# Attention: the squares for RMSNorm move from VectorE to ScalarE, and its factor is formed in three steps

## The chip, the cores and the metric

The kernel runs on one core of a Trainium2 chip. The metric is the device time in microseconds of one execution. PE is the matrix engine (TensorE), DVE is VectorE, ACT is ScalarE, POOL is GpSimd, and SP issues transfers.

## The reference

Two layers of a decoder run on 2048 prompt tokens and 64 sample tokens (8 sequences of 8), of 1024 features. The even layer projects its input, mixes half of it by pooling, and passes the other half through differential attention of four heads. The odd layer is gated linear attention. All is float32. The part that matters here is the attention of the prompt, its norm and its gate:

```python
p = softmax(sc)                          # [b, heads, 2, query, key], causal
a = p[:, :, 0] - lam_full * p[:, :, 1]
o = einsum('bhqk,bkhe->bqhe', a, v)      # 128 values a head
...
o = o * rsqrt(mean(o * o, -1) + 1e-5) * subln_w * (1 - lam_init)
mix = concat([pool_out * silu(pg), o * silu(ag)])
y = layer_norm(ALPHA * x + mix @ w_out)
```

## The kernel before

The program has three parts in time: the even layer's projection (`project_even`), the attention, and the odd layer (`Odd`). Float32 products with weights are done as three products of exact parts each (`mm3`, lines 51 to 53), with the parts formed by `split` (lines 40 to 45).

Attention (`class Attention`) goes by tiles of 128 queries. For each of 16 tiles t and each head h there is a unit, and `units` (line 572) lays them out: heads 0, then 1, then 2 and 3 in turn. A unit has two halves, and the second half (`pv`) comes two units after the first (`scores`), so that the engines overlap.

`scores` (line 459) has PE form the scores of two maps (the two softmaxes of differential attention) in pieces of up to 1024 keys, each in one of two pairs of banks of PSUM (lines 482, 483, and 485 for the causal mask). DVE takes the negated maximum of each row (487, or 490 for short tiles; 500 joins two pieces). ACT takes the exponential from the bank and gives the sums of the rows with it (502); only then is the bank free. If a map has two pieces (from tile 8 on), DVE adds their two sums (505), once for each map. Then DVE forms the factor c2 = -lambda s1 / s2 (509, 510) and e1 + c2 e2 (511), which is s1 times the wanted weights.

`pv` (line 516) has PE turn these weights in blocks of 128 x 128 (533), ACT copy them to SBUF (538), and PE multiply them with the values into one bank, `po` (526), of which there is a single buffer. Then comes the part that is changed. ACT copies o to SBUF (551). DVE squares that copy and sums the squares of a row (553), POOL copies s1 into a tile of two columns (555). After every second tile, `rms_scale` (line 1565) forms the norm's factor for both tiles of 128 queries. With s1 it takes on DVE a reciprocal r (1572), r squared (1573), times the sum of squares (1574), times 1/128 plus eps (1576), then, in `rsqrt`, a memset on DVE (1586) and the power -1/2 on POOL (1587), and at last times r on DVE (1579). POOL scales both tiles (560) and multiplies them with the gate (562). The gate was formed in `project_even`: the norm's weight times 1 - lambda_init (345) times silu (358, 359). Heads 0 and 1 go to memory from there (567); heads 2 and 3 stay in SBUF.

`weave` (line 367) puts other PE work between: with head 0 the pooling part of the output projection (`out_pool`: PE, then DVE at 636), with head 1 the attention of the samples (`Sample`), with heads 2 and 3 the attention part of the output projection (`out_attention`: transposes at 669, ACT at 673, DVE at 674, products, DVE at 712) and the LayerNorm of its rows, whose squares are summed on ACT (721), whose power is on POOL (1587), and whose scaling is three long POOL operations (733 to 735); 687 and 690 turn the rows for the odd layer. `rms_scale` without s1 also serves the samples (1502) and the odd layer, whose tiles also take the squares of o on ACT from a bank (1197).

Each engine has a queue that it works through in order. The order in the queues is laid down when the program is built, by a planner that goes through the emitted instructions with its own estimates of durations (`schedule_with_timeline_sim=True`, line 1685); the products of scores, the maxima and the exponentials are emitted with a raised priority (lines 477 and 498).

Of the kernel before, what the change touches and what calls it, by code (L numbers as in the profile page):

```python
# [36 lines left out]
def split(nc, raw, hi, lo, eng="act", lo_eng=None):  # L37
    """raw == hi + lo exactly, both float32r."""
    if eng == "act":
        h = nc.scalar.activation(hi, raw, AF.Copy)  # L40
    elif eng == "pool":
        h = nc.gpsimd.tensor_scalar(out=hi, in0=raw, scalar1=1.0, scalar2=1.0, op0=ALU.mult, op1=ALU.mult)
    else:
        h = nc.vector.tensor_copy(hi, raw)
    return h, (lo_eng or nc.vector).tensor_tensor(out=lo, in0=raw, in1=hi, op=ALU.subtract)  # L45


def mm3(nc, ps, lh, ll, rh, rl, n, first=True, last=True):
    """ps = sum over k of the float32 product of lhsT(k) and rhs(k), each given in two exact parts."""
    for k in range(n):  # L50
        nc.tensor.matmul(ps, lh(k), rh(k), start=(first and k == 0), stop=False)  # L51
        nc.tensor.matmul(ps, lh(k), rl(k), start=False, stop=False)  # L52
        nc.tensor.matmul(ps, ll(k), rh(k), start=False, stop=(last and k == n - 1))  # L53


class XSplit:
    """x^T in two exact float32r parts, resident, cut by token chunk"""
# [5 lines left out]
    def load(self, c, pool=None, before=None):  # L63
        """before: called with k ahead of rows k and k + 1; gives the last load"""
# [21 lines left out]
class Ring:  # L86
    """tiles of 4 KB a partition under one tag of a pool"""
# [16 lines left out]
class Weights:  # L104
    """units of 4 KB a partition, loaded and split as they are asked for"""
# [20 lines left out]
    def fm_pieces(self, src):  # L126
        """two blocks of features, loaded by two rows of w at a time: the products, and the loader"""
# [19 lines left out]
def layers(tc, d):  # L147
    """even layer: in-projection, rotary, pooling mixer; attention of the prompt with the output projection
    and the attention of the samples in between; the odd layer starts as the attention ends"""
# [3 lines left out]
    with ExitStack() as left:  # L153
# [10 lines left out]
        # the keys of attention, then the weights of the odd layer; raw loads  # L164
# [31 lines left out]
def project_even(tc, d, raw, W, slot):  # L196
    nc = tc.nc
    with ExitStack() as ctx:
# [20 lines left out]
        # rotated rows: block 0 holds the first halves (q then k), block 1 the second halves  # L219
# [23 lines left out]
        # pooling mixer  # L243
# [97 lines left out]
        # values and the attention gate, token-major  # L341
# [3 lines left out]
        nc.vector.tensor_scalar(out=gw, in0=gw, scalar1=1.0 - LAM_INIT, scalar2=None, op0=ALU.mult)  # L345
# [16 lines left out]
        # no table but this until the next Silu  # L362
# [19 lines left out]
class Attention:  # L382
    """differential attention of the prompt: a head after the other, tiles of 128 queries"""

    def __init__(self, tc, d, ctx, psf, keep):
# [16 lines left out]
        self.kst, self.vt, self.qs, self.sgs, self.oq = {}, {}, {}, {}, {}  # L402
# [8 lines left out]
        # 0 where key <= query (the row), else the lowest number  # L411
        nc.gpsimd.affine_select(out=self.mask, in_=self.mask, pattern=[[-1, 128]], compare_op=ALU.is_ge,
                                fill=-3.0e38, base=0, channel_multiplier=1)
        self.nlam = neg_lambda(tc, cst, self.raw, d)

# [9 lines left out]
    def load_kv(self, h, kc):  # L425
        """[k_hi; k_lo] of both maps of a head for 512 keys, and the values"""
# [17 lines left out]
    def load_q(self, h, qc):  # L444
        """[q_hi; q_hi] and [q_lo; q_lo] for 256 queries; their gates"""
# [13 lines left out]
    def scores(self, t, h):  # L459
        """e1 + c2 e2 in the first tile, s1 times the wanted weights; one chunk of up to 1024 keys a step"""  # L460
# [4 lines left out]
        # a tile takes both maps, or up to 1024 keys of one  # L465
# [4 lines left out]
        s = sm.tile([128, 2, 2], F32, tag="s", name=f"s{t}_{h}", bufs=6)  # L470
        es = [self.big.tile([128, NP], F32, tag="e", name=f"e{t}_{h}_{c}", bufs=5) for c in range(2)]
        for c in range(2):
# [25 lines left out]
            with self.tc.high_priority(300):  # L498
                if nt == 2:
                    nc.vector.tensor_tensor(out=nm[:, c, 0:1], in0=nm[:, c, 0:1], in1=nm[:, c, 1:2], op=ALU.min)  # L500
                for i, (m, p, o) in enumerate(pieces):
                    nc.scalar.activation(o, p, AF.Exp, bias=nm[:, m, 0:1],  # L502
                                         accum_out=s[:, m, i if npc > 1 else 0:][:, :1])
                if nt == 2:
                    nc.vector.tensor_tensor(out=s[:, c, 0:1], in0=s[:, c, 0:1], in1=s[:, c, 1:2], op=ALU.add)
            if c == 1:
                s1, s2 = s[:, 0, 0:1], s[:, 1, 0:1]
                c2 = sm.tile([128, 1], F32, tag="c2", name=f"c2{t}_{h}", bufs=6)
                nc.vector.reciprocal(out=c2, in_=s2)
                nc.vector.scalar_tensor_tensor(out=c2, in0=s1, scalar=self.nlam, in1=c2, op0=ALU.mult, op1=ALU.mult)  # L510
                nc.vector.scalar_tensor_tensor(out=es[0][:, :nk], in0=es[1][:, :nk], scalar=c2, in1=es[0][:, :nk],
                                               op0=ALU.mult, op1=ALU.add)
                self.cur = (es[0], s1)
            yield 2 * min(npc, 2) * max(w, 256) / 2.4

    def pv(self, t, h, a, s1):
        """o = (e1 + c2 e2) v, its RMSNorm (the factor s1 taken out there) and gate"""
# [27 lines left out]
        if q == 0:  # L545
            self.oq[h] = ((self.mixp if h >= 2 else self.rp).tile([128, 2, 128], F32, tag="oq", name=f"oq{t}_{h}",
                                                                       bufs=6 if h >= 2 else 4),
                          sm.tile([128, 2], F32, tag="ssq", name=f"ssq{t}_{h}"),
                          sm.tile([128, 2], F32, tag="s1q", name=f"s1q{t}_{h}"))
        oq, ssq, s1q = self.oq[h]  # L550
        nc.scalar.activation(oq[:, q, :], po, AF.Copy)  # L551
        sq = self.rp.tile([128, 128], F32, tag="sq", name=f"sqq{t}_{h}")
        nc.vector.scalar_tensor_tensor(out=sq, in0=oq[:, q, :], scalar=1.0, in1=oq[:, q, :], op0=ALU.mult,
                                       op1=ALU.mult, accum_out=ssq[:, q:q + 1])
        nc.gpsimd.tensor_scalar(out=s1q[:, q:q + 1], in0=s1, scalar1=1.0, scalar2=1.0, op0=ALU.mult, op1=ALU.mult)
        if q == 1:
            sc = rms_scale(self.tc, sm, ssq, 1.0 / 128, s1q, f"a{t}_{h}")
# [14 lines left out]
    def units(self, heads, after):  # L572
        """all tiles of queries of the given heads; the products with the values come two units later.
        after: the heads whose first loads are to be emitted on the way"""
# [29 lines left out]
def out_mm(nc, tile_, name, n, mh, ml, w, sink):  # L604
    """n tokens of mix @ w for four blocks of 128 features, in two halves of the columns"""
# [12 lines left out]
def out_pool(tc, d, A, W, slot):  # L618
    """z0 = alpha x + the pooling mixer's part of the output projection"""
# [22 lines left out]
def out_attention(tc, d, A, wp, op, sm):  # L642
    """y0 = LayerNorm(z0 + the attention's part of the output projection), and its transpose"""
# [60 lines left out]
class LayerNorm:  # L704
    """z <- LayerNorm(alpha z + p) g + b, rows of 1024; p comes in two halves"""
# [9 lines left out]
    def finish(self, to, urgent=False):  # L715
        """urgent: much waits for these rows"""
# [23 lines left out]
# as long as no gate's running sum over a block falls below this, a block's weights are formed at once  # L740
# [3 lines left out]
class Odd:  # L744
    """odd layer: in-projection and gates, gated linear attention, output projection"""

    def __init__(self, tc, d, ctx, keep):
        self.tc, self.d, self.ctx = tc, d, ctx
        self.raw = Ring(keep, "raw")
        # four units, two under either tag  # L750
# [10 lines left out]
    def start(self):  # L761
        """the first chunks of x^T"""
# [11 lines left out]
    def run(self):  # L774
# [15 lines left out]
        # the place of the first chunks of x^T: weights of the output projection, the first block of GLA  # L790
# [35 lines left out]
def project_odd(tc, d, O, cst, xp, slot, ident, steep):  # L826
# [25 lines left out]
    # the last chunks of x^T come when the first two are there for long  # L852
# [5 lines left out]
    # gates.  a = x w_ga comes as 32 rows (w_ga in two parts), three times over; with the rows of a split as  # L858
    # (hi, hi, lo) against the rows of w_gb as (hi, lo, hi), z = a w_gb takes a single pass
# [19 lines left out]
    def gates():  # L879
# [3 lines left out]
        for c, (t0, n) in enumerate(CH):  # L883
# [19 lines left out]
                # running sums, from every start of a block of 128 tokens (of a sequence, for the samples)  # L903
# [102 lines left out]
class Gla:  # L1006
    """gated linear attention by tiles of tokens, and the output projection"""
    first = ("cb1", "k1", "q1")

    def __init__(self, tc, d, ident, raw, gl):  # L1010
# [3 lines left out]
        # buffers taken in turn, as a pool's may not be on both sides of a branch  # L1014
# [37 lines left out]
    def inside(self, i, nb, fast, bank):  # L1052
        """q exp(cb), k exp(cb_last - cb) turned, exp(cb_last) and the weights inside, by blocks of a tile.
        fast: the weights from q exp(cb - cb_last) and k exp(cb_last - cb); else they come from weights_inside"""
# [19 lines left out]
        if fast:  # L1074
            # below 1e-18 only where the weights come from weights_inside in the end
# [22 lines left out]
    def two(self, key, r, src, eng):  # L1098
        """r[src] in two parts"""
# [3 lines left out]
    def run(self, fast):  # L1103
        """inside is done for the first two tiles, and the values of the first are split"""
# [5 lines left out]
    def run_in(self, ctx, fast):  # L1110
# [597 lines left out]
```

## Time and profile before

| What | Value |
|---|---|
| Three runs, us | 2243.64, 2237.99, 2245.49; median 2243.64 |
| Profiled execution | span 2236.4 us, the only time that it has |
| PE busy in it | 95% |
| DVE, ACT, POOL busy in it | 52%, 30%, 29% |
| Mean granted clock of PE | 0.984 |
| Attention in it | from about 585 to 1264 us |

A row of a group of instructions reads: line, engine, operation, tile written <- tiles read, sizes, count | busy us, mean ns of one | idle time of the engine just before them, and which engine, tile and line ended most of it. A row of the order of time reads: start, duration, engine, line, operation, tiles; in brackets the idle time before it and what ended that. A row of the waits reads: who waited <- for whom: us in total, how often, the longest. PEld stands for PE's loads of weights, which overlap its products.

### The profile page before, as it was taken

The page shows a single profiled execution, that of the slowest core. Times are in us where ns is not written, and L with a number is a line of the kernel's source. Part 1 is how long each engine was busy: PE and PEld are TensorE (multiplying, and loading weights), DVE is VectorE, ACT ScalarE, POOL GpSimd, SP SyncE. Part 2 cuts the span into 40 slices and gives each one's busy share as a digit, 9 for nine tenths or more (in the row PEclk, how much of TensorE's full clock was granted, in tenths as well). Part 3 has the DMA queues.
Part 4 walks back from the last instruction along what each step waited for, and adds up shares of the span by engine and source line. Part 5 has one row for each costly group of instructions (what it writes and reads, how often), then busy time and mean ns, then how long its engine had stood idle before and what let it go on. Part 6 is the DMA issues. An engine that isn't in the chain of part 4 may idle for free. (4 is left out here: it accounts for less than half of the span.)

```text
span 2236.4 us, 31590 instructions
## 1 busy us (share of the span) xinstructions
PE 2118.4 (95%) x11777; PEld 1751.4 (78%) x11777; DVE 1152.1 (52%) x2326; ACT 677.4 (30%) x1398; POOL 656.9 (29%) x702
## 2 busy tenths in 40 slices
PE   8999999999889999878989899999999997999987
PEld 7888888878678867767877779888888885877776
DVE  7445411110585676798777654810100117789994
ACT  2111000001443455655556311401111124333331
POOL 0000000003475533556543400000003333455664
PEclk9999999999899999999999999999999998999999
DMA  7311224231675489653322544321212246455522
GB/s 264 131 41 44 60 84 117 103 113 64 171 213 165 142 287 283 167 164 111 103 97 81 166 142 127 125 78 47 83 57 78 80 136 209 149 170 178 166 93 73
DMA packets 202596, 288.50 MB, mean 129 GB/s; under 512 B 30818, under 2 KB 121314, under 8 KB 202434
## 3 DMA queue, kind: packets, MB, share of 16 engines
q1 hardware_dynamic: 166594, 225.30, 33.0%
q0 software_dynamic: 12688, 43.00, 5.1%
q10 hardware_dynamic: 23152, 18.09, 2.4%
q8 instruction: 95, 1.56, 0.3%
q14 instruction: 67, 0.55, 0.1%
HBM read 183.95 MB, written 102.38 MB: 128 GB/s over the span
## 5 line engine op out<-in xcount | busy, mean ns | idle before, releaser
L51 PE MATMUL pm<-xh,wh 128*128 128x512 f32 (+2 forms) x640 | 225.3, 355 | 6.7 <-ACT xh L40 6.5
L52 PE MATMUL pm<-xl,wh 128*128 128x512 f32 (+2 forms) x640 | 226.5, 354 | 1.5 <-DVE xl L45 1.5
L53 PE MATMUL pm<-xh,wl 128*128 128x512 f32 (+2 forms) x640 | 226.2, 353 | 0.0
L53 PE MATMUL vt<-wk,yl 128*128 128x512 f32 (+1 forms) x544 | 211.4, 389 | 0.0
L52 PE MATMUL vt<-wk,yh 128*128 128x512 f32 (+1 forms) x544 | 211.3, 390 | 0.0
L51 PE MATMUL vt<-wk,yh 128*128 128x512 f32 (+1 forms) x544 | 208.8, 390 | 0.0
L502 ACT ACTIVATE e<-sc,nm 128x640 f32<-128x640 f32 (+11 forms) x192 | 164.9, 864 | 118.2 <-DVE nm L500 66.2
L949 POOL TENSOR_TENSOR ve<-ve,nw 128x512 f32<-128x512 f32 (+1 forms) x34 | 45.1, 1328 | 467.6 <-ACT ve L948 467.5
L359 POOL TENSOR_TENSOR et<-et,gw 128x512 f32<-128x512 f32 (+1 forms) x17 | 22.1, 1300 | 544.8 <-ACT et L358 544.8
L45 DVE TENSOR_TENSOR wk<-wr,wk 128x1024 fp32r<-128x1024 f32 x28 | 35.5, 1268 | 272.3 <-ACT wk L40 271.9
L487 DVE TENSOR_REDUCE nm<-sc 128x1 f32<-128x768 f32 (+7 forms) x160 | 156.7, 991 | 20.9 <-PE sc L483 12.7
L526 PE MATMUL po<-vt,aT 128*128 128x128 f32 x1088 | 156.1, 282 | 4.4 <-ACT oq L551 4.4
L482 PE MATMUL sc<-kst,qh 128*128 128x512 f32 (+9 forms) x352 | 134.5, 385 | 26.8 <-ACT e L502 26.0
L526 PEld LDWEIGHTS po<-vt,aT 128*128 128x128 f32 x1088 | 140.4, 197 | 10.4 <-ACT oq L551 4.8
L51 PEld LDWEIGHTS pm<-xh,wh 128*128 128x128 f32 x640 | 120.6, 189 | 22.6 <-ACT xh L40 6.5
L52 PEld LDWEIGHTS pm<-xl,wh 128*128 128x128 f32 x640 | 120.7, 189 | 18.5 <-DVE xl L45 2.7
L53 PEld LDWEIGHTS pm<-xh,wl 128*128 128x128 f32 x640 | 120.6, 189 | 16.9 <-DVE wl L45 0.4
L483 PE MATMUL sc<-kst,ql 128*128 128x512 f32 (+9 forms) x352 | 121.5, 348 | 0.7 <-DVE ql L45 0.7
L51 PEld LDWEIGHTS vt<-wk,yh 128*128 128x128 f32 (+1 forms) x544 | 100.4, 185 | 23.0
L53 PEld LDWEIGHTS vt<-wk,yl 128*128 128x128 f32 (+1 forms) x544 | 100.4, 185 | 23.0
L52 PEld LDWEIGHTS vt<-wk,yh 128*128 128x128 f32 (+1 forms) x544 | 100.4, 185 | 22.9
L52 PE MATMUL qm<-yl,wk 128*128 128x512 f32 (+2 forms) x320 | 113.8, 356 | 1.5 <-DVE yl L45 1.5
(354 smaller groups left out, 5100.2 us busy)
## 6 DMA issues: line engine op xcount, KB each, us to landing
sk<-in_cachek SPq DMA_DIRECT2D x64, 256.0 KB
sv<-in_cachev SPq DMA_DIRECT2D x64, 256.0 KB
wr<-in_w_tm SPq DMA_DIRECT2D x24, 512.0 KB
wr<-in_w_fm SPq DMA_DIRECT2D x22, 512.0 KB
wr<-in_w_out SPq DMA_DIRECT2D x16, 512.0 KB
zx<-in_x SPq DMA_DIRECT2D x32, 256.0 KB
kr<-k SPq DMA_DIRECT2D x32, 256.0 KB
qr<-q SPq DMA_DIRECT2D x64, 128.0 KB
```

What stands on the lines that cost most here:

```text
L45: return h, (lo_eng or nc.vector).tensor_tensor(out=lo, in0=raw, in1=hi, op=ALU.subtract)
L51: nc.tensor.matmul(ps, lh(k), rh(k), start=(first and k == 0), stop=False)
L52: nc.tensor.matmul(ps, lh(k), rl(k), start=False, stop=False)
L53: nc.tensor.matmul(ps, ll(k), rh(k), start=False, stop=(last and k == n - 1))
L359: nc.gpsimd.tensor_tensor(out=e[:n], in0=e[:n], in1=gw[:n], op=ALU.mult)
L482: nc.tensor.matmul(o, qh[:, c, qs], kst[:, ks], start=True, stop=False)
L483: nc.tensor.matmul(o, ql[:, c, qs], kst[:, ks], start=False, stop=k < npc - 1)
L487: nc.vector.tensor_reduce(out=nm[:, c, i:i + 1], in_=p[:, :, :w], op=ALU.max, axis=AX.XY, negate=True)
L502: nc.scalar.activation(o, p, AF.Exp, bias=nm[:, m, 0:1], accum_out=s[:, m, i if npc > 1 else 0:][:, :1])
L526: nc.tensor.matmul(po, s[:, 128 * j:128 * j + 128], vt[:, k0 + j, :], start=(k0 + j == 0), stop=(k0 + j == n - 1))
L949: nc.gpsimd.tensor_tensor(out=e[:n], in0=e[:n], in1=nw[:n], op=ALU.mult)
```

## The change

The sums of the rows now live in one tile for every two tiles of queries, `sums[h]`, of which there are eight buffers; ACT's sums of a single piece go right into it, and with two pieces one DVE addition joins the sums of both maps. The squares of o are taken by ACT from the bank `po`, behind its copy. POOL's copy of s1 is gone. The norm's factor is formed as (ssq + 128 eps s1^2)^-1/2: one DVE step for 128 eps s1^2, one DVE addition, and the power on POOL with a constant made once. The missing factor 128^1/2 is put into the weight of the gate, and the samples' norm is fitted to that. `rms_scale` no longer has the branch with s1.

```diff
+        self.half = cst.tile([128, 2], F32, name="half")
+        nc.vector.memset(self.half, -0.5)
...
-        nc.vector.tensor_scalar(out=gw, in0=gw, scalar1=1.0 - LAM_INIT, scalar2=None, op0=ALU.mult)
+        nc.vector.tensor_scalar(out=gw, in0=gw, scalar1=(1.0 - LAM_INIT) * 128 ** 0.5, scalar2=None, op0=ALU.mult)
...
+        if t % 2 == 0:
+            self.sums[h] = sm.tile([128, 2, 2], F32, tag="sum", name=f"sum{t}_{h}", bufs=8)
+        total = self.sums[h]
+        q = t % 2
...
-                                         accum_out=s[:, m, i if npc > 1 else 0:][:, :1])
+                                         accum_out=s[:, m, i:i + 1] if nt == 2 else total[:, m, q:q + 1])
+            if c == 1:
                 if nt == 2:
-                    nc.vector.tensor_tensor(out=s[:, c, 0:1], in0=s[:, c, 0:1], in1=s[:, c, 1:2], op=ALU.add)
-            if c == 1:
-                s1, s2 = s[:, 0, 0:1], s[:, 1, 0:1]
+                    nc.vector.tensor_tensor(out=total[:, :, q], in0=s[:, :, 0], in1=s[:, :, 1], op=ALU.add)
...
+        sq = self.rp.tile([128, 128], BF16, tag="sq", name=f"sqq{t}_{h}")
         nc.scalar.activation(oq[:, q, :], po, AF.Copy)
-        sq = self.rp.tile([128, 128], F32, tag="sq", name=f"sqq{t}_{h}")
-        nc.vector.scalar_tensor_tensor(out=sq, in0=oq[:, q, :], scalar=1.0, in1=oq[:, q, :], op0=ALU.mult,
-                                       op1=ALU.mult, accum_out=ssq[:, q:q + 1])
-        nc.gpsimd.tensor_scalar(out=s1q[:, q:q + 1], in0=s1, scalar1=1.0, scalar2=1.0, op0=ALU.mult, op1=ALU.mult)
+        nc.scalar.activation(sq, po, AF.Square, accum_out=ssq[:, q:q + 1])
         if q == 1:
-            sc = rms_scale(self.tc, sm, ssq, 1.0 / 128, s1q, f"a{t}_{h}")
+            s1 = total[:, 0, :]
+            sc = sm.tile([128, 2], F32, tag="rmo", name=f"rmo{t}_{h}")
+            nc.vector.scalar_tensor_tensor(out=sc, in0=s1, scalar=128 * EPS, in1=s1, op0=ALU.mult, op1=ALU.mult)
+            nc.vector.tensor_tensor(out=sc, in0=sc, in1=ssq, op=ALU.add)
+            nc.gpsimd.tensor_tensor(out=sc, in0=sc, in1=self.half[:, 0:2], op=ALU.pow)
...
-        sc = rms_scale(self.tc, pool, ssq, 1.0 / 128, None, "s")
+        sc = rms_scale(self.tc, pool, ssq, 1.0, 128 * EPS, "s")
```

More of the change, by code (lines that the diff above doesn't have):

```diff
@@ L401, in __init__ @@
         self.psf = psf
-        self.kst, self.vt, self.qs, self.sgs, self.oq = {}, {}, {}, {}, {}
+        self.kst, self.vt, self.qs, self.sgs, self.oq, self.sums = {}, {}, {}, {}, {}, {}
         self.done, self.pend, self.mix, self.over = -1, [], {}, False
@@ L469, in scores @@
         nm = sm.tile([128, 2, 2], F32, tag="nm", name=f"nm{t}_{h}", bufs=4)
-        s = sm.tile([128, 2, 2], F32, tag="s", name=f"s{t}_{h}", bufs=6)
+        if t % 2 == 0:
+            self.sums[h] = sm.tile([128, 2, 2], F32, tag="sum", name=f"sum{t}_{h}", bufs=8)
+        total = self.sums[h]
+        q = t % 2
+        s = sm.tile([128, 2, 2], F32, tag="s", name=f"s{t}_{h}", bufs=6) if nt == 2 else None
         es = [self.big.tile([128, NP], F32, tag="e", name=f"e{t}_{h}_{c}", bufs=5) for c in range(2)]
@@ L547, in pv @@
                                                                        bufs=6 if h >= 2 else 4),
-                          sm.tile([128, 2], F32, tag="ssq", name=f"ssq{t}_{h}"),
-                          sm.tile([128, 2], F32, tag="s1q", name=f"s1q{t}_{h}"))
-        oq, ssq, s1q = self.oq[h]
+                          sm.tile([128, 2], F32, tag="ssq", name=f"ssq{t}_{h}"))
+        oq, ssq = self.oq[h]
+        sq = self.rp.tile([128, 128], BF16, tag="sq", name=f"sqq{t}_{h}")
         nc.scalar.activation(oq[:, q, :], po, AF.Copy)
-        sq = self.rp.tile([128, 128], F32, tag="sq", name=f"sqq{t}_{h}")
-        nc.vector.scalar_tensor_tensor(out=sq, in0=oq[:, q, :], scalar=1.0, in1=oq[:, q, :], op0=ALU.mult,
-                                       op1=ALU.mult, accum_out=ssq[:, q:q + 1])
-        nc.gpsimd.tensor_scalar(out=s1q[:, q:q + 1], in0=s1, scalar1=1.0, scalar2=1.0, op0=ALU.mult, op1=ALU.mult)
+        nc.scalar.activation(sq, po, AF.Square, accum_out=ssq[:, q:q + 1])
         if q == 1:
-            sc = rms_scale(self.tc, sm, ssq, 1.0 / 128, s1q, f"a{t}_{h}")
+            s1 = total[:, 0, :]
[3 more added lines that the diff above has]
+            nc.gpsimd.tensor_tensor(out=sc, in0=sc, in1=self.half[:, 0:2], op=ALU.pow)
             sg = self.sgs[h, t // 2]
@@ L1197, in scale @@
                 nc.scalar.activation(j, p[:, h, :], AF.Square, accum_out=ssq[:, h:h + 1])
-            sc = rms_scale(tc, sm, ssq, 1.0 / 256, None, f"{u}g{i}")
+            sc = rms_scale(tc, sm, ssq, 1.0 / 256, EPS, f"{u}g{i}")
             m = wk.tile([128, 1024], F32, tag="mix", name=f"gm{i}")
@@ L1270, in samples @@
             nc.sync.dma_start(r["y0"], d["y0"][NP:T, :])
-            sc = rms_scale(tc, sm, ssq, 1.0 / 256, None, f"{u}gsm")
+            sc = rms_scale(tc, sm, ssq, 1.0 / 256, EPS, f"{u}gsm")
             for c in range(2):
@@ L1562, in neg_lambda, with rms_scale @@
     return nl
-def rms_scale(tc, pool, ssq, inv_n, s, name):
-    nc = tc.nc
+def rms_scale(tc, pool, ssq, inv_n, eps, name):
     P, n = ssq.shape
     o = pool.tile([128, 8], F32, tag="rmo", name=f"rmo{name}")[:P, :n]
-    if s is not None:
-        r = pool.tile([128, 8], F32, tag="rmr", name=f"rmr{name}")[:P, :n]
-        nc.vector.reciprocal(out=r, in_=s)
-        nc.vector.tensor_tensor(out=o, in0=r, in1=r, op=ALU.mult)
-        nc.vector.tensor_tensor(out=o, in0=o, in1=ssq, op=ALU.mult)
-        ssq = o
-    nc.vector.tensor_scalar(out=o, in0=ssq, scalar1=inv_n, scalar2=EPS, op0=ALU.mult, op1=ALU.add)
+    tc.nc.vector.tensor_scalar(out=o, in0=ssq, scalar1=inv_n, scalar2=eps, op0=ALU.mult, op1=ALU.add)
     rsqrt(tc, pool, o, name)
-    if s is not None:
-        nc.vector.tensor_tensor(out=o, in0=o, in1=r, op=ALU.mult)
     return o
```

9 lines of the change are left out of this document (5 added, 4 removed).

## The prediction

> **What bounds the kernel now.** I read the page first, then the busy time of each engine by stages, then who waited for whom in the attention stage, then the DVE and ACT groups there, and last the order of time around single stalls. The first view is the page.
>
> ```profile
> span 2236.4 us, 31590 instructions
> PE 2118.4 (95%) x11777; PEld 1751.4 (78%) x11777; DVE 1152.1 (52%) x2326; ACT 677.4 (30%) x1398; POOL 656.9 (29%) x702
> ```
>
> TensorE (PE) is busy for 95% of the span. Its program doesn't change, so the change is worth what it takes from PE's idle time, or adds to it. It touches attention only, from 585 to 1264 us, and the next view is that stretch: head 0 with the first output projection, head 1 with the samples, heads 2 and 3 with the second projection. Columns: length; PE, weight loads, DVE, ACT and POOL busy; clock, DMA share, GB/s.
>
> ```profile
> 585.00:780.00 195.00, 183.12 (x1011) 150.71 (x1011) 140.54 (x259) 88.14 (x199) 115.97 (x158) 0.97 0.65 184
> 780.00:968.00 188.00, 170.10 (x1650) 129.71 (x1649) 135.43 (x356) 112.48 (x281) 78.77 (x118) 0.96 0.80 246
> 968.00:1264.00 296.00, 262.82 (x1652) 223.09 (x1651) 223.44 (x471) 160.40 (x333) 152.54 (x160) 0.99 0.33 103
> sum 679.00, PE 616.03 PEld 503.52 DVE 499.41 ACT 361.02 POOL 347.28; mean PE 205.34 PEld 167.84 DVE 166.47 ACT 120.34 POOL 115.76
> ```
>
> PE is idle for 679.00 - 616.03 = 63 us here, all that the change can touch. DVE is busy for 74%, ACT for 53%. The waits of this stretch name who ended that idle time (us in total, times, longest).
>
> ```profile
> ACT e L502 <- DVE nm L500: 66.2, 38, 5.4
> PE sc L482 <- ACT e L502: 26.0, 23, 2.6
> PE tp L533 <- ACT aT L538: 6.7, 11, 1.1
> PE po L526 <- ACT oq L551: 4.4, 2, 4.0
> PE op L53 <- DVE ol L674: 3.1, 3, 1.6
> PE tp L533 <- DVE c L509: 2.2, 1, 2.2
> PE tp L533 <- DVE e L511: 1.3, 1, 1.3
> ```
>
> The largest item is a chain over three engines: a product of scores needs a bank (L482), the exponential on ACT frees it (L502), and that exponential was itself late for the row maximum on DVE (L500, 66.2 us of ACT's idle time). So DVE's queue comes first; PE stalls that DVE may have made late are 26.0 + 3.1 + 2.2 + 1.3 = 32.6 us.
>
> **The change, part by part.** *DVE.* These are the groups of that stretch that the change removes, or whose price it borrows (busy us, mean ns; then idle before).
>
> ```profile
> L553 DVE SCALAR_TENSOR_TENSOR sqq<-oq 128x128 f32<-128x128 f32 x64 | 27.2, 425 | 5.6 <-ACT oq L551 5.5
> L500 DVE TENSOR_TENSOR nm<-nm 128x1 f32<-128x1 f32 x64 | 26.5, 414 | 0.9
> L510 DVE SCALAR_TENSOR_TENSOR c<-s,nlam,c 128x1 f32<-128x1 f32 x64 | 23.3, 364 | 1.3
> L505 DVE TENSOR_TENSOR s<-s 128x1 f32<-128x1 f32 x64 | 21.7, 339 | 69.8 <-ACT e L502 69.7
> L1579 DVE TENSOR_TENSOR rmoa<-rmoa,rmra 128x2 f32<-128x2 f32 x31 | 15.5, 499 | 4.9 <-POOL rmoa L1587 4.9
> L1573 DVE TENSOR_TENSOR rmoa<-rmra 128x2 f32<-128x2 f32 x32 | 12.0, 379 | 0.6
> L1576 DVE TENSOR_SCALAR rmoa<-rmoa 128x2 f32<-128x2 f32 x31 | 9.2, 297 | 0.5 <-DVE rmoa L1574 0.3
> L1574 DVE TENSOR_TENSOR rmoa<-rmoa,ssq 128x2 f32<-128x2 f32 x32 | 7.3, 229 | 0.4
> L553 DVE DVE_READ_ACCUMULATOR sqq<-oq 128x1 f32 x64 | 5.2, 81 | 0.0
> L1572 DVE RECIPROCAL rmra<-s1q 128x2 f32<-128x2 f32 x32 | 5.0, 159 | 3.3 <-POOL s1q L555 3.1
> ```
>
> Gone are the squares (27.2 + 5.2), the five small steps of the norm (15.5 + 12.0 + 9.2 + 7.3 + 5.0), and half of L505, since the sums of both maps are added at once (10.9): 92.3 us. A memset for each pair goes too and isn't counted. New for each of 32 pairs are a small three-operand step, priced like L510 (364 ns), and an add, priced like L500 (414 ns): 24.9 us. DVE loses 67 of 499 us, 14%.
>
> What of it lies on PE's path? Two stalls in order of time:
>
> ```profile
> 1009.82 2.39 POOL L734 TENSOR_TENSOR oz<-oz,lng 128x1024 f32<-128x1024 f32 x1
> 1009.88 2.35 DVE L1579 TENSOR_TENSOR rmoa<-rmoa,rmra 128x2 f32<-128x2 f32 x1 [0.64 <-POOL rmoa L1587]
> 1013.56 0.50 PE L53 MATMUL op<-wh,ol 128*128 128x512 f32 x1 [1.14 <-DVE ol L674]
> ...
> 1027.19 2.36 POOL L735 TENSOR_TENSOR oz<-oz,lnb 128x1024 f32<-128x1024 f32 x1
> 1027.79 1.91 DVE L553 SCALAR_TENSOR_TENSOR sqq<-oq 128x128 f32<-128x128 f32 x1
> 1029.63 0.75 DVE L487 TENSOR_REDUCE nm<-sc 128x1 f32<-128x576 f32 x1
> 1030.67 0.74 ACT L502 ACTIVATE e<-sc,nm 128x576 f32<-128x576 f32 x1 [2.91 <-DVE nm L500]
> 1031.55 0.40 PE L482 MATMUL sc<-kst,qh 128*128 128x288 f32 x1 [0.66 <-ACT e L502]
> ```
>
> Here a step on two elements takes 2.35 us, and one on 128 takes 1.91 us: each ends as a long POOL operation ends. Behind it stand the maximum (L487), the exponential, and PE. Both DVE steps are removed. I went through PE's stalls for those with a removed step directly in front of the late one. There are nine, 9.3 us in all; these are the first and the last.
>
> ```profile
> 624.06 0.50 PE L482 MATMUL sc<-kst,qh 128*128 128x512 f32 x1 [0.69 <-ACT e L502]
> ...
> 1149.12 0.50 PE L53 MATMUL op<-wh,ol 128*128 128x512 f32 x1 [0.38 <-DVE ol L674]
> ```
>
> Each counts for no more than the removed step held DVE: 0.3, 1.1, 0.4, 1.1, 0.7, 0.9, 1.0, 0.4 and 0.4 us, **6.2 us** gained. A check from the other side: 14% of the 32.6 us is 4.4. Lower end: a stretch may pass to the next small step on two SBUF tensors (L500 or the new add), and then only the plain duration is saved; with 0.3 us (the mean of L1576) for each of the nine, 2.7 us. Upper end: all nine stalls, 9.3 us.
>
> The Trainium skill, SBUF — State Buffer (section "Who interferes with whom"), says that a DVE instruction with two SBUF inputs and a POOL instruction that reads SBUF share one read interface, and that the later one is blocked until the earlier has finished. By that rule the reduction L487 (one input, PSUM) inherits no wait, while L500 does, as at the stall of 1.1 us in the list, so that the gain would be 5.1 us. The rows above agree with the rule so far.
>
> *ACT.* The copy of o stays and a Square with its accumulator read comes behind it, 64 times. Its price is taken from the Square of the odd layer, of 256 columns from a bank:
>
> ```profile
> 1889.42 0.36 ACT L1197 ACTIVATE gj<-go 128x256 bf16<-128x256 f32 x1
> ...
> 1889.78 1.04 ACT L40 ACTIVATE gvh<-gv 128x1024 fp32r<-128x1024 f32 x1
> ```
>
> ```profile
> 1043.48 0.27 ACT L551 ACTIVATE oq<-po 128x128 f32<-128x128 f32 x1
> 1043.64 0.79 ACT L502 ACTIVATE e<-sc,nm 128x640 f32<-128x640 f32 x1
> 1044.32 0.21 ACT L502 ACTIVATION_READ_ACCUMULATOR e<-sc,nm 128x1 f32 x1
> ```
>
> The next instruction starts 0.36 us after the 256-column Square. The 128-column copy L551 takes 0.27, 0.09 less than that Square, so 0.36 - 0.09 = 0.27 us of ACT's queue for each; the upper end is the two durations laid end to end, 0.27 + 0.21 = 0.48. That is 17 to 31 us more on ACT, 53% to some 57%. At 1043.48 one sees what hurts: the copy stands right ahead of an exponential for which PE then waits. I find eight stalls with L551 right in front of the ACT instruction that PE needs, or PE waiting for the bank of o itself; first and last:
>
> ```profile
> 947.79 0.50 PE L482 MATMUL sc<-kst,qh 128*128 128x512 f32 x1 [0.82 <-ACT e L502]
> ...
> 1250.03 0.44 PE L533 MATMUL tp<-ident,e 128*128 128x128 f32 x2 [0.76 <-ACT aT L538]
> ```
>
> Eight by 0.27 is **2.2 us** lost; by 0.48 it would be 3.8. The bank of o (one buffer) comes free later by about as much, but only two stalls hang on it, both among the eight. I take 0.27, since the neighbours show that an accumulator read overlaps its activation.
>
> *Rest.* POOL loses 64 copies of s1, and with them the waits for the sums of DVE in its queue; no stall of PE in the list above was ended by POOL, so I count nothing. DVE's new add waits for the Square (the old square waited 5.5 us for the copy), and behind it the maxima can queue, but in every second tile only: nothing either way. The power on POOL now feeds POOL directly; the return over DVE (L1579) is in the nine. The gate weights' constant, the samples' scale and the odd layer issue the same operations as before.
>
> **Sum:** -6.2 + 2.2 = -4.0 us. It is made against the profiled execution, whose 2236.4 us lie 7.2 us under the median of the runs shown, so I carry the difference over: 2243.64 - 4.0 = **2239.6 us**. Own range: from -9.3 + 2.2 to -2.7 + 3.8, that is 2236.5 to 2244.7. About 0.3% of the time, 6.7 us, is what a measurement can tell here.
>
> **The rivals.**
>
> *Relief beyond the nine stalls (chance 0.37).* DVE is the first queue of the chain, and a queue's waiting falls faster than its load: with load over idle share as the measure, 0.736/0.264 = 2.8 becomes 0.636/0.364 = 1.75 (an estimate from the busy times), 37% less. Of 32.6 us that is 12.1; less 2.2, some 10 us: 2233.7 us, or about 2231 where POOL also blocks less. For it: 66.2 us of ACT's idle time behind L500. Against it: only 26.0 us of this reached PE, and several of those stalls have ACT alone or a DMA behind them.
>
> *ACT takes DVE's place (0.13).* The order is laid down at build time. If the Squares come to stand in front of exponentials and copies for which PE waits, at all 23 + 11 + 2 = 36 places where ACT releases PE, that is 36 x 0.27 = 9.7 us, with DVE's relief eaten by steps that inherit the port's wait: 2253.3 us. It decides from 25 such places on (25 x 0.27 = 6.7) with no relief beside. Against it: ACT idles for 47% of the stage. The Trainium skill, ScalarE: Activation LUTs (section "Rules for kernel authors"), says that a plain multiplication belongs on VectorE, not on ScalarE; by that rule this rival is what should be expected. Here the removed DVE square took 425 ns on average, so the trace does not bear it out for this size.
>
> *The planner's order (0.06).* With other durations the whole order of attention is laid anew; no row prices that, and I spread it evenly on both sides.
>
> That Square would need another table of ACT's than the exponentials is no rival with a chance: the LayerNorm of heads 2 and 3 already runs a Square (line 721) between them, and the ACT groups of the stretch hold no table load.
>
> **How the numbers follow.** The forecast has 0.44 and lies within 0.3%. Faster by over 0.3%: 0.37 and half of the planner's case, 0.40. Slower: 0.13 and the other half, 0.16. The range of 2227 to 2249 takes in the forecast's own range, most of the relief case, and the milder half of the ACT case.
>
> **What would show it.** In the profile after, attention should have DVE busy for some 67 us less and ACT for 17 to 31 us more; PE's idle time there should be near 59 us of the 63; L482 behind L502 should fall from 26.0 to about 22, and steps like those at 1009.88 and 1027.79 should be gone. The Square should take near 0.27 us with a read of 0.2 us behind it. I am wrong if L482's wait falls under 15 us (the relief), if L533 and L526 wait clearly more for ACT than 6.7 and 4.4 us (ACT took over), or if DVE's small steps L500 and L510 stretch more than before, so that its busy time hardly falls.

## The result, and the profile after

The changed kernel takes 2261.18 us (median of four runs, 2258.11 to 2262.70), the kernel before 2244.18 beside it: a ratio of 1.0073 with a 95% interval of 1.0055 to 1.0092. It is slower by some 17 us, where 4 us of gain were forecast.

The page of the kernel after, its first lines:

```profile
span 2255.9 us, 31353 instructions
...
PE 2124.9 (94%) x11777; PEld 1759.3 (78%) x11777; DVE 1106.4 (49%) x2039; ACT 689.4 (31%) x1526; POOL 645.3 (29%) x638
```

DVE and POOL have less to do, as intended, and ACT a little more; yet PE, with the same 11777 products, is busy for 6.5 us longer, and the span is 19.5 us longer. The groups of DVE and ACT that are new or answer to those shown of before (585 to 1281 us, where attention now ends):

```profile
L516 DVE SCALAR_TENSOR_TENSOR c<-sum,nlam,c 128x1 f32<-128x1 f32 x64 | 30.2, 472 | 1.2
L507 DVE TENSOR_TENSOR nm<-nm 128x1 f32<-128x1 f32 x64 | 18.9, 296 | 0.7
L513 DVE TENSOR_TENSOR sum<-s 128x2 f32<-128x2 f32 x32 | 18.0, 564 | 37.4 <-ACT e L509 37.4
L559 ACT ACTIVATE sqq<-po 128x128 bf16<-128x128 f32 x63 | 17.6, 279 | 0.0
L559 ACT ACTIVATION_READ_ACCUMULATOR sqq<-po 128x1 f32 x63 | 13.4, 212 | 0.0
L564 DVE SCALAR_TENSOR_TENSOR rmo<-sum 128x2 f32<-128x2 f32 x32 | 12.7, 396 | 1.9 <-ACT e L509 1.8
L565 DVE TENSOR_TENSOR rmo<-rmo,ssq 128x2 f32<-128x2 f32 x31 | 8.1, 260 | 9.5 <-ACT sqq L559 9.4
```

Gone with the squares, the norm's five steps and all of the old L505 are 27.2 + 5.2 + 49.0 + 21.7 = 103.1 us; come are 18.0 + 12.7 + 8.1 = 38.8. With c2 (now L516) up by 6.9 and the joining of maxima (now L507) down by 7.6, the durations of all these add up to 65 us less, where the forecast said 67. DVE's busy time falls by less, from 521.63 to 476.94 us (the two sums further down), that is by 44.7, because the durations of neighbouring steps overlap.

The waits of the same stretch, who waited for whom:

```profile
ACT e L509 <- DVE nm L507: 68.5, 28, 8.5
...
PE sc L489 <- ACT e L509: 33.3, 30, 3.2
...
PE tp L540 <- ACT aT L545: 17.2, 17, 2.9
```

In the kernel before these rows had 66.2, 26.0 and 6.7 us. ACT waits for the maxima as long as ever though DVE has less to do, and PE waits for ACT 18 us longer in the other two rows. To see where, I cut both traces at places of equal PE work (the same products done). Length, PE, weight loads, DVE, ACT, POOL, clock, DMA share, GB/s; first the kernel before, then the one after:

```profile
1097.00:1301.00 204.00, 186.00 (x1127) 156.07 (x1126) 136.73 (x267) 100.11 (x194) 86.82 (x86) 1.00 0.36 114
sum 716.00, PE 651.52 PEld 531.87 DVE 521.63 ACT 369.86 POOL 359.30; mean PE 217.17 PEld 177.29 DVE 173.88 ACT 123.29 POOL 119.77
```

```profile
1100.00:1321.00 221.00, 194.63 (x1128) 162.06 (x1127) 129.19 (x201) 101.83 (x218) 88.74 (x78) 0.96 0.33 104
sum 736.00, PE 657.98 PEld 539.46 DVE 476.94 ACT 382.15 POOL 348.72; mean PE 219.33 PEld 179.82 DVE 158.98 ACT 127.38 POOL 116.24
```

The sums go from 585 us on. Over all of it PE's idle time grew from 716.00 - 651.52 = 64.5 to 736.00 - 657.98 = 78.0 us, and its busy time by 6.5: together the 20 us. Of this, 17 us lie in one stretch, the last third of heads 2 and 3: 8.4 us of idle time (26.4 for 18.0) and 8.6 us of busy time, for the same products at a granted clock of 0.96 for 1.00. One stall from there, in order of time:

```profile
1165.12 0.36 PE L490 MATMUL sc<-kst,ql 128*128 128x448 f32 x1
...
1166.36 2.35 POOL L743 TENSOR_TENSOR oz<-oz,lng 128x1024 f32<-128x1024 f32 x1
...
1167.04 1.69 DVE L564 SCALAR_TENSOR_TENSOR rmo<-sum 128x2 f32<-128x2 f32 x1
...
1168.65 1.08 DVE L494 TENSOR_REDUCE nm<-sc 128x1 f32<-128x896 f32 x1
...
1169.37 2.33 POOL L744 TENSOR_TENSOR oz<-oz,lnb 128x1024 f32<-128x1024 f32 x1
...
1169.65 2.06 DVE L516 SCALAR_TENSOR_TENSOR c<-sum,nlam,c 128x1 f32<-128x1 f32 x1
1171.64 0.15 DVE L507 TENSOR_TENSOR nm<-nm 128x1 f32<-128x1 f32 x1
...
1171.82 1.01 ACT L509 ACTIVATE e<-sc,nm 128x896 f32<-128x896 f32 x1 [3.79 <-DVE nm L507]
...
1172.97 0.66 PE L489 MATMUL sc<-kst,qh 128*128 128x448 f32 x1 [3.19 <-ACT e L509]
...
1173.43 0.57 PE L490 MATMUL sc<-kst,ql 128*128 128x448 f32 x1
```

The small step that the change adds (L564) takes 1.69 us, the factor c2 (L516) 2.06, and each ends as a long operation of POOL's LayerNorm ends. Behind them stand the maximum, the exponential, and PE for 3.19 us. No Square of o is in this chain. And the same product L490 that took 0.36 us before the stall takes 0.57 behind it.

### The profile page after: what moved, and what is told of

The parts are those of the page before. It is cut to its first block, busy times and chain, and to the rows that moved or that the text cites. A ratio compares the mean times of both kernels' runs of the same rounds, so it can differ in the third digit from the quotient of the medians.

```text
span 2255.9 us, 31353 instructions
## 1 busy us (share of the span) xinstructions
PE 2124.9 (94%) x11777; PEld 1759.3 (78%) x11777; DVE 1106.4 (49%) x2039; ACT 689.4 (31%) x1526; POOL 645.3 (29%) x638
## 5 line engine op out<-in xcount | busy, mean ns | idle before, releaser
L494 DVE TENSOR_REDUCE nm<-sc 128x1 f32<-128x768 f32 (+7 forms) x160 | 156.6, 992 | 57.7 <-PE sc L490 45.3
L53 PEld LDWEIGHTS pm<-xh,wl 128*128 128x128 f32 x640 | 120.6, 188 | 17.2 <-DVE wl L45 0.9
L490 PE MATMUL sc<-kst,ql 128*128 128x512 f32 (+9 forms) x352 | 124.7, 357 | 0.0
L52 PEld LDWEIGHTS vt<-wk,yh 128*128 128x128 f32 (+1 forms) x544 | 100.4, 185 | 22.9
```

The source lines that it names most:

```text
L490: nc.tensor.matmul(o, ql[:, c, qs], kst[:, ks], start=False, stop=k < npc - 1)
L494: nc.vector.tensor_reduce(out=nm[:, c, i:i + 1], in_=p[:, :, :w], op=ALU.max, axis=AX.XY, negate=True)
```

## The experiments

Ratios are to the kernel before, run beside each on the same chip. Two theories stood first. *The Square*: 64 Squares with their reads, on an engine that PE waits for, cost the time themselves. *The order*: the planner, seeing other operations, lays the queues down anew, and this order is worse.

**One part alone, and other plans.** The first kernel is the changed one with the squares back on DVE, by the edit shown; the second is the kernel before with nothing changed but the Square on ACT.

```diff
-        sq = self.rp.tile([128, 128], BF16, tag="sq", name=f"sqq{t}_{h}")
         nc.scalar.activation(oq[:, q, :], po, AF.Copy)
-        nc.scalar.activation(sq, po, AF.Square, accum_out=ssq[:, q:q + 1])
+        sq = self.rp.tile([128, 128], F32, tag="sq", name=f"sqq{t}_{h}")
+        nc.vector.scalar_tensor_tensor(out=sq, in0=oq[:, q, :], scalar=1.0, in1=oq[:, q, :], op0=ALU.mult,
+                                       op1=ALU.mult, accum_out=ssq[:, q:q + 1])
```

> The changed kernel, with the squares of o back on DVE from the copy in SBUF; the joint sums and the short norm factor stay. Theory A (the Square on ACT, in front of the copies and exponentials that PE waits for, is the cause): the loss goes away and the relief of DVE is left, 2236 to 2243 us, with the wait of the transposes for ACT's copies back near 7 us from 17. Theory B (the planner's new order costs the time, whatever the operations are): the order is new here too, so the time can land anywhere between 2235 and 2262 us and needs have nothing to do with where the squares are.

> The kernel before, with nothing changed but the squares of o, which ACT takes from the bank behind its copy. Theory A: the whole loss, 2255 to 2265 us, and the wait of the transposes for ACT's copies near 17 us. Theory B: anywhere between 2235 and 2262 us.

Measured: 2232.75 us, 0.9960 [0.9943, 0.9976], and 2263.66 us, 1.0096 [1.0074, 1.0118]. The loss comes with the Square and with nothing else in the change; by itself this speaks for both theories. The next two change no operation, only the constant that paces the work woven in, so that the planner lays another order:

```diff
-HEAD_COST = 76000.0
+HEAD_COST = 77000.0
```

> The kernel before with the weight of the weaving set from 76000 to 77000, so that the work between the units of attention is emitted a little earlier or later; every instruction stays as it is, only the order changes. Theory A: the time stays within 4 us of the kernel before, 2240 to 2248 us. Theory B: it moves by 8 us or more in either direction, as order alone decides.

> The changed kernel with the same shift of the weaving (77000 for 76000), all instructions as in the changed kernel. Theory A: it stays at 2257 to 2265 us, since the Squares stay on ACT. Theory B: it moves by 8 us or more, perhaps below 2250 us.

Measured: 2241.24 us, 0.9985 [0.9971, 0.9999] for the kernel before, and 2256.16 us, 1.0060 [1.0040, 1.0080] for the changed one. By the ratios this order moves either kernel by some 3 us, hardly beyond the intervals, and not by 17.

**Orders held.** Here PE's products are chained, without semaphores, in the order of another kernel (the operations of PE are the same in all); the planner lays the other queues around them, so that an order of PE is always tested together with these queues. Of the edit, the parts that make the chain:

```diff
+def chain(tc, insts, why):
+    for a, b in zip(insts, insts[1:]):
+        tc.add_manual_dep(b, a.name, mybir.DependencyInfo(mybir.DependencyClass.NoSync, mybir.DependencyReason.DATA),
+                          reason=why)
...
+    order = decode(ORDER_PE)
...
+    chain(tc, [pe[k] for k in order], "pe order")
```

> The kernel before with the squares of o on ACT from the bank, PE and ACT held by issue-order edges to the very order of the kernel before; each Square stands directly behind its copy. Theory A1 (each Square delays ACT's own queue, and PE behind it): most of the loss stays, 2255 to 2265 us. Theory A2 (the Squares cost little by themselves, but the planner answers them with a worse order on PE): the loss goes away, 2240 to 2250 us.

> The changed kernel, all its operations, with PE held to the order of the kernel before; ACT, DVE and POOL as the planner lays them. A1: 2250 to 2260 us, as the Squares' delay stays and DVE's relief of some 9 us is kept. A2: 2230 to 2242 us.

> The kernel before, all its operations (squares on DVE, the long norm factor), with PE held to the order of the changed kernel. A1: the order is worth no more than the 5 us by which another order moved the kernel before, 2238 to 2250 us. A2: 2255 us or more, as the new order on PE is what costs.

Measured: 2257.71 us, 1.0067 [1.0041, 1.0093]; 2234.38 us, 0.9958 [0.9946, 0.9971]; 2288.27 us, 1.0208 [1.0176, 1.0240]. The last two turn the result round. The changed kernel, all of its operations in place, beats the kernel before once PE has the old order, and the kernel before, with no Square of o on ACT, loses 44 us in the new one. Waits of PE from 585 to 1281 us with the changed operations in the old order, and to 1300 us with the old operations in the new order (lines are shifted by the added helper: the first row of each is the scores, the second the transposes):

```profile
PE sc L538 <- ACT e L558: 27.7, 18, 4.2
PE tp L589 <- ACT aT L594: 12.6, 14, 2.7
```

```profile
PE sc L531 <- ACT e L551: 38.3, 30, 5.3
PE tp L582 <- ACT aT L587: 17.3, 17, 2.7
PE tp L582 <- DVE c L559: 8.5, 1, 8.5
```

From the old order to the new one, the two rows in which ACT releases PE grow together by 22.9 us with the old operations (32.7 to 55.6) and by 10.2 with the changed ones (40.3 to 50.5). The changed operations add 7.6 us to them in the old order and take 5.1 off in the new one. The 8.5 us of the last row are a single stall behind DVE, a part of the 44. The first kernel of the three held ACT's order too, with the Square straight behind the copy, and seemed to speak for the Square. Its waits have one row that the others lack:

```profile
PE tp L582 <- ACT aT L587: 26.1, 11, 14.6
```

A single stall of 14.6 us is nearly the whole loss. So it was run again with only PE held to the order of before (the first of the next four). The second is the changed kernel in the order of before with each Square issued twice, which writes the same values again. The third holds the changed kernel with squares on DVE to the changed kernel's order, and the fourth the changed kernel to the order planned for squares on DVE. All use such a chain; the second adds a line:

```diff
         nc.scalar.activation(sq, po, AF.Square, accum_out=ssq[:, q:q + 1])
+        nc.scalar.activation(sq, po, AF.Square, accum_out=ssq[:, q:q + 1])
```

> The operations of the run with only the Square moved (2263.66 us), with PE held to the order of before; ACT's order is left to the planner, unlike in the run that held both (2257.71) and had one stall of 14.6 us. If PE's order is the cause, it comes back to before: 2238 to 2247. If the Square's own place on ACT costs the 20 us, it stays at 2255 to 2265.

> The changed kernel with every Square issued twice (64 more Squares, the second writes the same values), PE held to the order of before. It prices the Square directly, against 2234.4 us for the same with one Square. If only some stalls have it in front (my eight, 0.27 us each): +2 us, 2236 to 2238. If ACT is short of time everywhere (64 times 0.27 to 0.48): +17 to +31, 2251 to 2265.

> The changed kernel with its squares back on VectorE (2232.75 us in its own order), with PE held to the order of the changed kernel. No Square of o is on ACT. If PE's order is the cause: 2255 to 2285, as slow as the changed kernel or slower. If the Square on ACT is the cause: within 5 us of 2232.75.

> The changed kernel, all its operations, with PE held to the order that the planner made for the version with squares on VectorE. If PE's order is the cause: 2228 to 2238, some 25 us under the changed kernel. If the Square on ACT is the cause: 2255 to 2265.

Measured: 2243.76 us, 0.9983 [0.9968, 0.9998]; 2267.44 us, 1.0098 [1.0074, 1.0122]; 2270.80 us, 1.0115 [1.0093, 1.0138]; 2241.20 us, 0.9979 [0.9963, 0.9994]. The first shows that the 14.6 us came from holding ACT. Together the runs give a table of operations by PE's order (own plans in italics):

| Operations | order of before | order of after | order with squares on DVE |
|---|---|---|---|
| before | *1* | 1.0208 | |
| before, Square on ACT | 0.9983 | | |
| changed | 0.9958 | *1.0073* | 0.9979 |
| changed, squares on DVE | | 1.0115 | *0.9960* |

Every entry of the middle column is slow, every other one is not. The run that held ACT's order as well (1.0067, with PE in the old order) is not in the table; it shows that PE's order alone does not fix the time, and that the queues laid around it count too. Read along the columns, moving the squares to ACT under a held order is worth -0.2% (old order), -0.4% (new) and +0.2% (third): from -9 to +4 us, each uncertain by 3 to 6 us, what DVE is spared included.

The doubled Square is the exception. It costs 1.0098 - 0.9958 = 1.4%, 31 us for 64 more, or 0.49 us each. That is as much as the two durations end to end (0.28 + 0.21), but it is not shown to be their price: the planner seldom puts the second Square behind the first. In 59 of 64 cases other work of ACT stands between, and the second begins 0.6 to 3.1 us after the first. The longest of them:

```profile
1160.88 0.28 ACT L578 ACTIVATE sqq<-po 128x128 bf16<-128x128 f32 x1
...
1161.13 0.60 ACT L564 ACTIVATE aT<-tp 128x512 f32<-128x512 f32 x1
1161.60 0.97 ACT L528 ACTIVATE e<-sc,nm 128x832 f32<-128x832 f32 x1
...
1163.94 0.32 ACT L579 ACTIVATE sqq<-po 128x128 bf16<-128x128 f32 x1
```

The bank of o is held for so long. PE's waits for that bank, with one Square in the old order, then with two, and the whole of attention with two:

```profile
PE po L582 <- ACT sqq L608: 1.5, 1, 1.5
```

```profile
PE po L552 <- ACT sqq L579: 11.9, 7, 5.3
```

```profile
585.00:1329.00 744.00, 671.51 (x4473) 547.92 (x4472) 471.45 (x831) 400.67 (x1081) 346.76 (x381) 0.94 0.54 162
```

With one Square the same work takes 716.00 us, 656.17 of them busy, at a clock of 0.96. Of the 28 us between these two profiles, 12.7 are idle time of PE, most of it the single bank of o held longer (10.4), and 15.3 are the same products at a lower clock. What a second Square right behind the first would cost, this run does not show.

**The bank of o.** To see whether a bank held longer is already behind the 17 us, the Square takes the copy in SBUF, so that the bank is free after the copy:

```diff
-        nc.scalar.activation(sq, po, AF.Square, accum_out=ssq[:, q:q + 1])
+        nc.scalar.activation(sq, oq[:, q, :], AF.Square, accum_out=ssq[:, q:q + 1])
```

> The changed kernel with the Square on ACT reading the copy of o in SBUF in place of the bank, so that the bank of o is free again after the copy as before. A3 (the single bank of o, held longer by the Square, is what PE loses by): 2240 to 2250 us. A1: 2255 to 2265 us, since ACT's queue is as full as with the bank.

Measured: 2260.60 us, 1.0081 [1.0051, 1.0112]. The time stays, but this does not price the bank, since the kernel has a plan of its own: in the profiles PE's order parts from that of the changed kernel at the start of attention, and the Square begins 0.3 to 4.8 us after the copy, where 0.15 to 0.17 is the rule in the changed kernel (63 of 64). The waits of the changed kernel itself say more. From 585 to 1321 us they hold no row in which PE waits for a Square, so that the bank is not seen to cost it anything.

**Where in the order.** The changed kernel with PE's order put together from two, cut at the 625th product of scores. The chain is the same, and only its list differs: in the first it has the products up to the cut in the order of after and then all others in the order of before, in the second the two are exchanged.

> The changed kernel with PE held to its own order for the first 625 products of scores (up to about 1072 us, the first two thirds of heads 2 and 3) and to the order of before from there. If the loss lies in the order of the last third, as the time at equal PE work says: 2232 to 2241. If it lies earlier and only shows late: 2252 to 2262.

> The reverse: the order of before up to the same place, then the changed kernel's own. If the loss lies in the order of the last third: 2252 to 2262. If it lies earlier: 2232 to 2241.

Measured: 2245.67 us, 0.9993 [0.9981, 1.0005], and 2265.25 us, 1.0086 [1.0063, 1.0108]. The order of the last third carries most of the loss: it is worth 18 us taken out of the new order (1.0073 to 0.9993) and 29 put into the old one (0.9958 to 1.0086). It is not all: the new order in the first two thirds alone costs 8 us (0.9958 to 0.9993), and the run missed the 2232 to 2241 us expected. The stretch of equal work, first with the old order there, then with the new one:

```profile
1100.00:1306.00 206.00, 188.27 (x1118) 158.24 (x1117) 128.34 (x206) 102.03 (x216) 94.02 (x76) 0.98 0.36 112
```

```profile
1102.00:1322.00 220.00, 193.53 (x1130) 161.19 (x1131) 129.88 (x201) 102.37 (x218) 89.18 (x78) 0.97 0.33 105
```

The same operations take 206 or 220 us there: 17.7 or 26.5 us of idle time, and 5.3 us more of busy time.

**A rule or a draw.** Whether the planner answers Squares on ACT with a worse order as a rule, four more plans had to tell: the changed kernel at 78000, the kernel before at 78000 and 73000, the changed one with squares on DVE at 77000.

```diff
-HEAD_COST = 76000.0
+HEAD_COST = 78000.0
```

> The changed kernel with the constant that paces the fill work at 78000 for 76000, which only makes the planner lay another order. If plans with the Squares on ACT are worse as a rule: 2250 to 2266, as in all four so far (2256 to 2264). If after's order was a chance draw: as likely under 2246 as above.

> The kernel before with the same constant at 78000. If plans without the Squares are better as a rule: 2236 to 2247. If plans scatter by chance over 2233 to 2264: as likely above 2250 as below.

> The kernel before with the constant at 73000. The same two theories as for 78000: 2236 to 2247 as a rule, or anywhere from 2233 to 2264 by chance.

> The changed kernel with squares back on VectorE and the constant at 77000. If such plans are better as a rule: 2228 to 2240. If the 2232.75 us of its first plan was a lucky draw: 2240 to 2264.

Measured: 2250.72 us, 1.0017 [1.0002, 1.0033]; 2244.24 us, 1.0003 [0.9986, 1.0020]; 2260.84 us, 1.0079 [1.0051, 1.0107]; 2246.77 us, 0.9999 [0.9984, 1.0015]. Five plans with the Squares on ACT now stand at 1.0017 to 1.0096 (mean 1.0065), six without at 0.9960 to 1.0079 (mean 1.0004). The kernel before, with a constant moved by 4%, can be as slow as the changed one, and the changed one can come within 0.2%. So the draw is shown to be large; that plans with the Squares are worse on average (0.6%) is likely but rests on few plans that overlap, and why the planner would make them so stays open.

The fastest versions, both faster than both kernels, are the changed kernel in the old order (0.9958) and the changed kernel with squares on DVE (0.9960). Their intervals overlap. The second had luck with its plan: with the constant at 77000 the same operations take 0.9999.

## Why the prediction was wrong

**The step that failed** was this one: "With other durations the whole order of attention is laid anew; no row prices that, and I spread it evenly on both sides." It had a chance of 0.06 and no size. The runs put the size at 26 us for the changed operations (0.9958 to 1.0073), 44 us for the old ones and 35 us for those with squares on DVE, each time with the operations unchanged and only PE's order, and the queues that the planner lays around it, different. The whole sum of the direct terms, 4.0 us, was smaller than the spread of what it left out.

**DVE's load** (-67 us, 14%) was too large as relief. The durations of the groups fell by 65 us, but I set their sum against a busy time in which overlaps count once. A removed square held the queue for less than its two durations, here 0.22 us for 0.28 + 0.08 (kernel before):

```profile
1006.03 0.28 DVE L553 SCALAR_TENSOR_TENSOR sqq<-oq 128x128 f32<-128x128 f32 x1
1006.24 0.08 DVE L553 DVE_READ_ACCUMULATOR sqq<-oq 128x1 f32 x1
1006.25 0.16 DVE L509 RECIPROCAL c<-s 128x1 f32<-128x1 f32 x1
```

DVE's busy time over attention fell by 44.7 us, 9%.

**The nine stalls and the Squares** (-6.2 + 2.2; the nine figures listed add up to 6.3): they can be compared only under the old order, where the change gives 0.9958 [0.9946, 0.9971], 6 to 12 us of gain. The sign is the forecast's; that the gain comes the forecast's way is not shown, and the profile of that run speaks against it. PE's idle time from 585 to 1301 us is 716.00 - 656.17 = 59.8 us there, 4.7 less than before:

```profile
585.00:968.00 383.00, 353.16 (x2622) 280.02 (x2622) 246.80 (x453) 204.30 (x540) 184.10 (x234) 0.94 0.72 214
...
sum 716.00, PE 656.17 PEld 536.42 DVE 467.89 ACT 382.93 POOL 351.24; mean PE 218.72 PEld 178.81 DVE 155.96 ACT 127.64 POOL 117.08
```

But the three rows in which PE waits for ACT (scores, transposes, the bank of o) have grown from 37.1 to 41.8 us; the scores' row, which should have fallen from 26.0 to 22, has 27.7. And PE's busy time takes the 4.7 us back, at a lower clock (0.94 in the first of the three stretches, where the kernel before had 0.97). So attention takes as long as before in this execution, and all of the 5.3 us by which it is shorter lie behind 1301 us, in the odd layer (first the kernel before):

```profile
1301.00:2236.40 935.40, 893.33 (x4508) 738.20 (x4506) 442.82 (x879) 238.27 (x468) 263.48 (x216) 0.98 0.35 117
```

```profile
1301.00:2231.10 930.10, 891.83 (x4505) 737.47 (x4503) 440.65 (x879) 238.21 (x468) 262.45 (x216) 0.98 0.36 117
```

Whether the medians gain in the same place, two profiles don't show. That the gain has the forecast's sign may be luck.

**A stretch that passes on** was named as the lower end and happened: the new L564 and c2 took over the wait behind POOL in the stall at 1172.97, and the mean of c2 rose from 364 to 472 ns. The Trainium skill, SBUF — State Buffer ("Who interferes with whom"), gives the two engines one shared interface for a DVE step with two inputs in SBUF; the reduction L494 between them, with one input in PSUM, took 1.08 us although L744 started within it, so this trace agrees.

**The Square's price** (0.27 us and a read of 0.2) was right: 279 and 212 ns. ACT's busy time over attention grew by 12.3 us (369.86 to 382.15), less than the 17 to 31 forecast. The argument "ACT idles for 47% of the stage" fits the -9 to +4 us of one Square; the doubled Squares don't decide it, as their cost is for the most part a held bank and a lower clock.

**The rival "ACT takes DVE's place"** gave 2253.3 us, nearest to the result, and its sign came true: L540's wait for ACT rose from 6.7 to 17.2 us. But its mechanism is not the cause. With the same Squares and the old order the loss is gone, and without them the new order has the same 17.3 us in that row. (With them the old order has 12.6, so a part of the growth does come with the changed operations.) My sign could not tell a longer queue from a worse order. The rule cited for this rival, of the Trainium skill, ScalarE: Activation LUTs ("Rules for kernel authors"), is not borne out for one Square of this size: -9 to +4 us under held orders.

**The clock** was in no term. Of the 20 us of the profiled executions, 13.5 are idle time and 6.5 the same products done more slowly.

## What to carry to other kernels

Where a planner lays down the queues, a change of operations is also a new draw of the order: before a gain of a few microseconds is worked out from stalls, measure how far the time moves when only a pacing constant moves (here, for the kernel before, from 0.2% below to 0.8% above). Separate the two by holding the bounding engine's order while the operations change, in both directions, and remember that the other queues move with it. Durations that overlap don't add up to the time that an engine is spared. And a row that names who was waited for does not say whether the work or its place is to blame.

## What the runs showed of the hardware

A stall of PE can be paid twice. Around the stall at 1172.97 of the kernel after, the clock before it and behind it:

```profile
1165.00:1168.00 3.00, 3.00 (x20) 2.44 (x20) 2.22 (x4) 1.81 (x4) 3.00 (x4) 1.00 0.42 126
1173.10:1176.40 3.30, 3.30 (x11) 2.63 (x12) 1.89 (x3) 1.72 (x6) 0.36 (x1) 0.50 0.39 159
```

After 3.19 us without work, 3.3 us ran at half the clock, so the stall cost 1.7 us more. The Trainium skill, TensorE: Matmul & The Clock Gate ("Part 1: The HAM clock gate (the "warmup" mystery)"), says that the clock is halved after an idle window of some 3.4 us and that these windows run freely. The length of the slow stretch agrees; but here a stall shorter than a window was enough. Not every stall of 2 us has this effect: in the kernel before, the clock stayed at 1.00 behind this one.

```profile
1163.94 0.41 PE L669 MATMUL otp<-oident,om 128*128 128x128 f32 x2 [2.02 <-DMA om<-mixa]
```

```profile
1164.00:1167.40 3.40, 3.29 (x24) 2.87 (x25) 2.75 (x2) 1.98 (x5) 3.32 (x2) 1.00 0.28 81
```

It is how an order with longer stalls can lose more than their sum.
